# Turns by way of DRAM, and the forget gate's and the convolution's side work in smaller steps, in a hybrid decoder layer on one core

## The chip, the core and the metric

The kernel runs on one core of a Trainium2 chip. The metric is device time in microseconds (us), from launch to end. Three runs of the kernel before took 882.16, 876.36 and 881.53 us, a median of 881.53 us. One more execution was taken with the hardware profiler; all traces and tables here are of that one.

## The reference

One decoder layer, 256 tokens, model width 2048, all in float32:

```
h = rmsnorm(x)
c, b, xa, za, q, f, iv, og, ga, gb = split(h @ W_in)      # 8 x 1024 and 2 x 2048 columns
ya = b * causal_conv3(c * xa) * silu(za)                  # per column, three taps over tokens
lb = clip(lb_all, 0, 1 - 1e-6)
log_f = logaddexp(log(max(lb, 1e-30)), log1p(-lb) + log_sigmoid(f))
k  = (1 - lb) * sigmoid(-f)
o  = gated linear recurrence over tokens (silu(q), k, iv, log_f)   # 8 heads of 128, blocks of 64 tokens
yb = rmsnorm_per_head(o) * gain * silu(og)
m  = sigmoid(ga) * (ya @ W_a) + sigmoid(gb) * (yb @ W_b)
x  = x + m @ W_o
x  = x + sigmoid(rmsnorm(x) @ W_pg) * (p @ W_pp)
out = rmsnorm(x)
```

The result must be as exact as float32. TensorE has a fast format with fewer bits, so each factor is split into a high part (rounded to the fast format) and a low part (what is left), and a product is three matmuls: high x high, low weight x high, high weight x low activation.

## The kernel before

**Stream of weights.** All weights are read once, in 292 pieces called chunks here: 128 partitions x 1024 values, 512 KB. Two chunks come in one 1 MB transfer into a `raw` tile (three buffers, `load`, L104), issued on SyncE's queue. For each chunk `split` makes two halves: ScalarE copies `raw` to `whi` (L117, 1.05 us), then VectorE subtracts, `wlo = raw - whi` (L118, 1.24 us). Both have four buffers. TensorE then runs 12 matmuls of 128x512 on the chunk (`product`, L796 to L798), one every 0.227 us, 2.72 us in all. So each of the three engines has a job per chunk, and the next weights can be split only when the chunk four places earlier has been used up.

**Groups.** Chunks belong to groups, each with one product of two PSUM tiles (2 x 128 tokens, 512 columns). Their order: for j = 0 and 1 the groups f, q, iv, og, c, xa, za, b of 8 chunks each (chunks 0 to 127); for j = 0 to 3 ga and gb of 8, and A and B of 4 (128 to 223); O for j = 0 to 3 (224 to 255); then for j = 0 to 3 PP of one chunk and PG of 8.

**Side work.** After a group, its epilogue (`ep_f`, `ep_q`, `ep_xa`, ...) works on the result with VectorE, ScalarE, GpSimd and DMAs while TensorE is on the next groups. Epilogues are Python generators: the main loop advances each of them by one `yield` per chunk, and so a `yield` puts what stands behind it one chunk later. A scheduler then orders the instructions of each engine; within an engine they run strictly in that order, weight halves and side work in one queue. The recurrence itself (`hgrn`) is advanced in the same way.

**Turns.** A group's result has tokens on partitions. 18 tiles need columns on partitions instead: f, q, xa, b and yb (the recurrence's result) for j = 0 and 1; m (the merged branches) and x1 (the residual) for j = 0 to 3. VectorE's transpose turns 32x32 blocks within one quarter of the partitions, so the quarters must first be exchanged. `turned` (L178 to L196) does this with 16 transfers of 32 KB (32 partitions x 256 values) from SBUF to SBUF, issued one by one on SyncE's queue (L187), four or eight per `yield`; `lag` yields later comes the transpose (L194, 1.24 us). The weight loads are on the same queue and wait behind them.

**Forget gate.** `ep_f` turns f, takes two sigmoids of the turned tile (L239, L240), then for each of four heads scales `sn` into `kT` (L251) and takes three logarithms, with the scale `one` and the bias `low` of the lower bound inside the activation (L256); two of the three write 128x128 values, one 128x2. The scan (L259) sums the logarithms over 64 tokens; `tot` (L263, L264) and the `y` of the recurrence (L364) follow on VectorE. A sigmoid and a logarithm live in different tables of ScalarE; each change is a table load (1.28 us). q's epilogue, the next group, brings two sigmoids (L209) and two products (L226).

**Convolution.** `ep_xa` makes, for each of four blocks of 128x256, one VectorE multiplication for the last tap (L490) and seven shifted additions (L496), one block per `yield`.

**Late stages.** The four m tiles feed the groups O (`mh`, `ml`, L553 and L554); GpSimd adds the two merged halves (L549). `ep_o` adds O's result to the residual `xs` (L561), and turns it to x1 (`xh`, `xl`, L151 and L152) for PG.

Of the kernel before, what the change touches and what calls it, by code (L numbers as in the profile page):

```python
# [15 lines left out]
P = 128  # L16
# [28 lines left out]
def hybrid_kernel(ctx, tc, xT, x, pT, prm, gfin, masks, w_in, w_a, w_b, w_o, w_pg, w_pp, out):  # L45
# [4 lines left out]
    small = ctx.enter_context(tc.tile_pool(name="small", bufs=1))  # L50
    ps = ctx.enter_context(tc.tile_pool(name="ps", bufs=1, space=PSUM))
    big = ctx.enter_context(tc.tile_pool(name="big", bufs=1))


    pools, closers = {}, {}
# [21 lines left out]
    def t4(tag="t4", bufs=None):  # L77
        bufs = bufs or {"tmp1": 8, "tmp2": 5, "tmp3": 5}[state["tmp"]]
        return pools[state["tmp"]].tile([P, 1024], F32, tag=tag, bufs=bufs, name=nm(tag))
# [4 lines left out]
    def sc(n, tag="sc", bufs=12):  # L84
        return small.tile([P, n], F32, tag=tag, bufs=bufs, name=nm(tag))
# [89 lines left out]

        return ap.rearrange("p (b c t e) -> p t c b e", b=4, c=4, t=NT)[:, t]

    def turned(src, dst, step, lag):  # L178

        u = t4()
        for n in range(16):
            a, b = n % 4, n // 4
            nc.sync.dma_start(  # L187
                out=u[32 * b : 32 * b + 32, a * T : (a + 1) * T], in_=src[32 * a : 32 * a + 32, b * T : (b + 1) * T]
            )
            if n % step == step - 1:  # L190
                yield
        for _ in range(lag):
            yield
        nc.vector.transpose(  # L194
            out=dst.rearrange("p (k a e) -> p a k e", a=4, e=32), in_=u.rearrange("p (a k e) -> p a k e", a=4, e=32)
        )  # L196


    def scaled(psum, dst, turn=False):
# [34 lines left out]
    def ep_f(j, psum):  # L234
        fl = t4()
        scaled(psum, fl, True)
        yield from turned(fl, fl, 4, 3)
        sg, sn = t4(), t4()
        nc.scalar.activation(out=sg, in_=fl, func=AF.Sigmoid)  # L239
        nc.scalar.activation(out=sn, in_=fl, func=AF.Sigmoid, scale=-1.0)  # L240
        yield


        kT, lf, last = t4("kT", 1), t4(), sc(8, "lfl", 2)
        lv, sv = segments(lf), segments(sg)
        lsv = last.rearrange("p (h s) -> p h s", h=4)
        nc.gpsimd.memset(lv[:, :, 1, :, 0:1], 0.0)
        for h in range(4):
            s = slice(h * T, (h + 1) * T)
            one, low = (state[n][:, j * 4 + h : j * 4 + h + 1] for n in ("oml", "lbm"))  # L250
            nc.scalar.activation(out=kT[:, s], in_=sn[:, s], func=AF.Identity, scale=one)  # L251
            for to, fr in (
                (lv[:, h, 0], sv[:, h, 0]), (lv[:, h, 1, :, 1:], sv[:, h, 1, :, : SCAN - 1]),
                (lsv[:, h], sv[:, h, 1, :, SCAN - 1]),
            ):
                nc.scalar.activation(out=to, in_=fr, func=AF.Ln, scale=one, bias=low)  # L256
        yield
        b, tot = t4("b", 1), sc(16, "tot", 2)
        nc.vector.tensor_tensor_scan(  # L259
            out=b, data0=carry, data1=lf, initial=0.0, op0=ALU.mult, op1=ALU.add  # L260
        )
        bv, tv = segments(b), tot.rearrange("p (h k s) -> p h k s", h=4, k=2)
        nc.vector.tensor_copy(out=tv[:, :, 0], in_=bv[:, :, 0, :, SCAN - 1])  # L263
        nc.vector.tensor_tensor(  # L264
            out=tv[:, :, 1], in0=bv[:, :, 1, :, SCAN - 1],
            in1=last.rearrange("p (h s) -> p h s", h=4), op=ALU.add,
        )
        state["kT", j], state["b", j], state["tot", j] = kT, b, tot

    def ep_q(j, psum):  # L270
        sg, qt = t4(), t4()
        sig(psum, sg)
        plain_times(psum, sg, qt)
        qT = t4("qT", 1)
        yield from turned(qt, qT, 4, 3)
        state["qT", j] = qT

    def ep_iv(j, psum):
        v = t4("v", 1)
# [4 lines left out]
    def ep_og(j, psum):  # L284
        sg, o = t4(), t4("og", 1)
        sig(psum, sg)
        times(psum, sg, o)
        state["og", j] = o
        yield
        yield  # L290
        yield from hgrn(j)

    def hgrn(j):
# [144 lines left out]
        ss = sc(8, "ssh", 2)  # L438
        for n in range(8):
            t, h = n // 4, n % 4  # L440
            nc.scalar.activation(
                out=sq[:, n * P : (n + 1) * P], in_=o[t][:, h * P : (h + 1) * P], func=AF.Square,
                scale=state["rstd1"][:, t : t + 1], accum_out=ss[:, n : n + 1],
            )
# [5 lines left out]
        yield  # L450
        for n in range(8):
            t, h = n // 4, n % 4
            nc.scalar.activation(
                out=spread(sq, t)[:, h], in_=yb[:, n * P : (n + 1) * P].rearrange("p (b e) -> p b e", e=32),
                func=AF.Identity, scale=rh[:, n : n + 1],
            )
        yield from turned(sq, yb, 8, 3)
        for i in range(4):
            k = j * 4 + i
            put(state["ybT"], k, yb[:, i * T : (i + 1) * T], gain(PRM_GHG, k))  # L460
# [13 lines left out]
    def ep_xa(j, psum):  # L474
        cx = t4()
        plain_times(psum, state["c", j], cx)
        cxT = cx
        yield from turned(cx, cxT, 4, 3)
        cv = t4("cv", 1)
        for h in range(2):  # L480
            for i in range(2):
                n = h * 2 + i
                k = j * 4 + n
                d, s = cv[:, n * T : (n + 1) * T], cxT[:, n * T : (n + 1) * T]

                def w(tap):
                    c = PRM_CONV + tap * 8 + k
                    return prm_t[:, c : c + 1]

                nc.vector.tensor_scalar(out=d, in0=s, scalar1=w(2), scalar2=None, op0=ALU.mult)  # L490

                for tap, to, fr, n_ in (
                    (1, 1, 0, P - 1), (1, P, P + 1, P - 1), (1, T - 1, P - 1, 1),
                    (0, 2, 0, P - 2), (0, P, P + 2, P - 2), (0, T - 2, P - 1, 1), (0, T - 1, P - 2, 1),
                ):
                    nc.vector.scalar_tensor_tensor(  # L496
                        out=d[:, to : to + n_], in0=s[:, fr : fr + n_], scalar=w(tap), in1=d[:, to : to + n_],
                        op0=ALU.mult, op1=ALU.add,
                    )
                yield  # L500
        state["cv", j] = cv

    def ep_za(j, psum):
# [6 lines left out]
    def ep_b(j, psum):  # L510
        bz = t4()
        plain_times(psum, state["zs", j], bz)
        ya = bz
        yield from turned(bz, ya, 8, 3)
        nc.vector.tensor_tensor(out=ya, in0=state["cv", j], in1=ya, op=ALU.mult)
        yield
        hi, lo = (x[:, j * 4 : (j + 1) * 4, :].rearrange("p k t -> p (k t)") for x in state["yaT"])
        nc.scalar.activation(out=hi, in_=ya, func=AF.Copy)
        nc.vector.tensor_tensor(out=lo, in0=ya, in1=hi.bitcast(F32), op=ALU.subtract)
# [21 lines left out]
    def ep_bb(j, psum):  # L541
        ga, gb = state["ga", j], state["gb", j]
        for t in range(NT):
            s = slice(t * CW, (t + 1) * CW)
            nc.vector.tensor_tensor(out=gb[:, s], in0=gb[:, s], in1=psum[t], op=ALU.mult)  # L545
        m = t4()
        for t in range(NT):
            s = slice(t * CW, (t + 1) * CW)
            nc.gpsimd.tensor_tensor(out=spread(m, t), in0=blocks(ga[:, s]), in1=blocks(gb[:, s]), op=ALU.add)  # L549
        yield from turned(m, m, 8, 2)  # L550
        k = j * 4
        hi, lo = (x[:, k : k + 4, :].rearrange("p k t -> p (k t)") for x in state["mT"])
        nc.scalar.activation(out=hi, in_=m, func=AF.Copy)  # L553
        nc.vector.tensor_tensor(out=lo, in0=m, in1=hi.bitcast(F32), op=ALU.subtract)  # L554

    def ep_o(j, psum):
        xs = state["x"]
        src = t4()
        for t in range(NT):
            d = xs[:, t, j * CW : (j + 1) * CW]  # L560
            nc.vector.tensor_tensor(out=d, in0=d, in1=psum[t], op=ALU.add)  # L561
            nc.scalar.activation(  # L562
                out=src[:, t * CW : (t + 1) * CW], in_=d, func=AF.Square,
                accum_out=state["ss2"][:, t * 4 + j : t * 4 + j + 1],
            )
        x1 = src
        for t in range(NT):
            nc.scalar.activation(  # L568
                out=spread(x1, t), in_=blocks(xs[:, t, j * CW : (j + 1) * CW]), func=AF.Copy
            )  # L570
        yield from turned(x1, x1, 8, 2)
        for c in range(4):
            put(state["x1T"], j * 4 + c, x1[:, c * T : (c + 1) * T], gain(PRM_GPLE, j * 4 + c))
        if j == 3:
            tot = sc(2, "tot2", 1)
            nc.vector.tensor_reduce(
                out=tot, in_=state["ss2"].rearrange("p (t j) -> p t j", t=NT),
                axis=mybir.AxisListType.X, op=ALU.add,
            )
            state["rstd2"] = rsqrt_of(tot, NT, D, "r2")  # L580
# [374 lines left out]
```

## Time and profile before

| what | value |
|---|---|
| profiled execution, its own time | 880.19 us |
| span, first to last instruction | 878.4 us |
| mean granted TensorE clock | 0.982 |
| busy: TensorE, VectorE, ScalarE, GpSimd | 836.3, 527.6, 443.3, 77.0 us |
| idle time of TensorE between matmuls, and after the last | 33.5 and 8.5 us |
| instructions of VectorE, ScalarE | 592, 584 |
| bytes read from and written to HBM | 161.39 and 2.10 MB |
| DMA busy share of 16 engines, main queue | 55.5% |

The matmuls are a stream that is nearly always busy; the holes in it are these (start in the span, length, what ended the wait):

| place | start, length (us) | ended by | what stood before it |
|---|---|---|---|
| start | 0.00 1.45; 4.96 0.53; 8.87 1.11; 10.48 0.22 | warm-up, whi, wlo | first loads |
| A | 29.85 1.10; 31.69 0.53 | whi, wlo | scaling of f (L201) on ScalarE |
| B | 62.00 4.17; 67.39 3.00 | whi, wlo | first f: sigmoids, logarithms, scan |
| C | 227.83 1.04; 229.38 0.76; 236.10 0.28 | whi, wlo | 32 transfers of two turns, b and yb |
| D | 260.70 4.11; 266.02 3.00 | whi, wlo | second f |
| E | 426.19 1.00; 427.69 0.76; 434.45 0.24 | whi, wlo | as C, for j = 1 |
| F | 625.61 0.56 | wlo | a turn of m |
| G | 686.13 1.38; 688.24 0.53 | mh, ml | last turn of m, ahead of O |
| H | 715.81 4.24; 720.78 0.53 | whi, wlo | first turn of x1 |
| K | 785.37 2.27; 788.37 0.53 | xh, xl | last turn of x1, ahead of PG |

The granted clock is half of full speed from 65.7 to 76.0 us, 263.7 to 274.0, 721.1 to 724.5 and 789.4 to 792.8.

How to read the lines: an instruction group is named by line, engine, operation, and tiles out<-in. A row of a timeline is start in us, duration, engine, line, operation, tiles, count, and in brackets the idle time before and what ended it. A row of waits is the waiting engine and line, what it waited for, and total us, times, longest. A row of windows is the stretch, its length, then the busy us of PE, PEld, DVE, ACT and POOL (with instruction counts), the granted clock, the DMA share and GB/s. PE is TensorE, DVE VectorE, ACT ScalarE, POOL GpSimd, and SPq the queue of SyncE, on which most transfers are issued.

### The profile page before, as it was taken

The page shows a single profiled execution, that of the slowest core. Times are in us where ns is not written, and L with a number is a line of the kernel's source. Part 1 is how long each engine was busy: PE and PEld are TensorE (multiplying, and loading weights), DVE is VectorE, ACT ScalarE, POOL GpSimd, SP SyncE. Part 2 cuts the span into 40 slices and gives each one's busy share as a digit, 9 for nine tenths or more (in the row PEclk, how much of TensorE's full clock was granted, in tenths as well). Part 3 has the DMA queues.
Part 4 walks back from the last instruction along what each step waited for, and adds up shares of the span by engine and source line. Part 5 has one row for each costly group of instructions (what it writes and reads, how often), then busy time and mean ns, then how long its engine had stood idle before and what let it go on. Part 6 is the DMA issues. An engine that isn't in the chain of part 4 may idle for free. (4 is left out here: it accounts for less than half of the span.)

```text
span 878.4 us, 10033 instructions
## 1 busy us (share of the span) xinstructions
PE 836.3 (95%) x3753; PEld 687.4 (78%) x3753; DVE 527.6 (60%) x592; ACT 443.3 (50%) x584; POOL 77.0 (9%) x76
## 2 busy tenths in 40 slices
PE   8988999999988999999999999999999979989996
PEld 5766888888776888888788888888788768868885
DVE  7445586985646586985645545545545546655572
ACT  7673474445473474445443443443443445555552
POOL 1000032201000032200001001001001000001110
PEclk9997999999997999999999999999999999999999
DMA  9755645643654745643664753753753856554542
GB/s 334 292 197 172 235 164 180 209 166 101 224 204 141 265 153 188 212 155 111 229 242 139 273 200 128 275 200 123 269 200 131 338 198 250 192 201 160 207 153 96
DMA packets 39793, 173.59 MB, mean 198 GB/s; under 512 B 7616, under 2 KB 16832, under 8 KB 21568
## 3 DMA queue, kind: packets, MB, share of 16 engines
q1 hardware_dynamic: 39312, 172.39, 55.5%
q8 instruction: 29, 0.48, 0.2%
q10 hardware_dynamic: 432, 0.56, 0.2%
q14 instruction: 20, 0.16, 0.1%
HBM read 161.39 MB, written 2.10 MB: 186 GB/s over the span
## 5 line engine op out<-in xcount | busy, mean ns | idle before, releaser
L118 DVE TENSOR_TENSOR wlo<-raw,whi 128x1024 fp32r<-128x1024 f32 (+1 forms) x294 | 361.6, 1242 | 250.7 <-ACT whi L117 246.9
L117 ACT ACTIVATE whi<-raw 128x1024 fp32r<-128x1024 f32 (+1 forms) x294 | 305.4, 1052 | 319.7 <-PE g L798 272.8
L796 PE MATMUL g<-whi,xh 128*128 128x512 f32 (+1 forms) x912 | 355.6, 392 | 15.3 <-ACT whi L117 13.1
L797 PE MATMUL g<-wlo,xh 128*128 128x512 f32 (+1 forms) x912 | 356.0, 390 | 9.5 <-DVE wlo L118 9.4
L798 PE MATMUL g<-whi,xl 128*128 128x512 f32 (+1 forms) x912 | 354.4, 389 | 0.5 <-DVE xl L152 0.5
L796 PEld LDWEIGHTS g<-whi,xh 128*128 128x128 f32 x912 | 172.9, 190 | 52.9 <-ACT whi L117 16.1
L797 PEld LDWEIGHTS g<-wlo,xh 128*128 128x128 f32 x912 | 173.0, 190 | 48.7 <-DVE wlo L118 14.7
L798 PEld LDWEIGHTS g<-whi,xl 128*128 128x128 f32 x912 | 173.1, 190 | 35.5 <-DVE xl L152 1.0
L796 PE MATMUL g<-whi,mh 128*128 128x512 f32 x128 | 50.2, 393 | 5.6 <-ACT whi L117 4.2
L797 PE MATMUL g<-wlo,mh 128*128 128x512 f32 x128 | 50.7, 396 | 0.5 <-DVE wlo L118 0.5
L798 PE MATMUL g<-whi,ml 128*128 128x512 f32 x128 | 50.6, 395 | 0.5 <-DVE ml L554 0.5
L194 DVE STREAM_TRANSPOSE t<-t 128x1024 f32<-128x1024 f32 x16 | 19.9, 1241 | 39.6 <-DMA t<-t 39.6
L549 POOL TENSOR_TENSOR t<-ga,gb 128x512 f32<-128x512 f32 x8 | 14.1, 1789 | 255.5 <-DVE gb L545 192.8
L796 PEld LDWEIGHTS g<-whi,mh 128*128 128x128 f32 x128 | 24.2, 190 | 11.5 <-ACT whi L117 4.7
L797 PEld LDWEIGHTS g<-wlo,mh 128*128 128x128 f32 x128 | 24.4, 191 | 6.1 <-DVE wlo L118 1.0
L798 PEld LDWEIGHTS g<-whi,ml 128*128 128x128 f32 x128 | 24.5, 191 | 6.0 <-DVE ml L554 1.0
L796 PE MATMUL g<-whi,yaTh 128*128 128x512 f32 x64 | 24.9, 389 | 0.0
L797 PE MATMUL g<-wlo,yaTh 128*128 128x512 f32 x64 | 24.9, 389 | 0.0
L798 PE MATMUL g<-whi,yaTl 128*128 128x512 f32 x64 | 24.9, 389 | 0.0
L796 PE MATMUL g<-whi,ybTh 128*128 128x512 f32 x64 | 24.9, 389 | 0.0
L797 PE MATMUL g<-wlo,ybTh 128*128 128x512 f32 x64 | 24.9, 389 | 0.0
L798 PE MATMUL g<-whi,ybTl 128*128 128x512 f32 x64 | 24.9, 389 | 0.0
(147 smaller groups left out, 539.7 us busy)
## 6 DMA issues: line engine op xcount, KB each, us to landing
raw<-in_w_in SPq DMA_DIRECT2D x91, 1024.0 KB, 5.0
raw<-in_w_o SPq DMA_DIRECT2D x16, 1024.0 KB, 5.3
raw<-in_w_pg SPq DMA_DIRECT2D x16, 1024.0 KB, 4.9
t<-t SPq DMA_DIRECT2D x288, 32.0 KB, 1.9
raw<-in_w_a SPq DMA_DIRECT2D x8, 1024.0 KB, 5.0
raw<-in_w_b SPq DMA_DIRECT2D x8, 1024.0 KB, 5.0
raw<-in_w_in SPq DMA_DIRECT2D x9, 512.0 KB, 7.8
t<-in_xT SPq DMA_DIRECT2D x8, 256.0 KB, 7.5
```

The source lines that it names most:

```text
L117: nc.scalar.activation(out=hi[:, s], in_=src[:, s], func=AF.Copy)
L118: nc.vector.tensor_tensor(out=lo[:, s], in0=src[:, s], in1=hi[:, s].bitcast(F32), op=ALU.subtract)
L194: nc.vector.transpose(out=dst.rearrange("p (k a e) -> p a k e", a=4, e=32), in_=u.rearrange("p (a k e) -> p a k e", a=4, e=32))
L549: nc.gpsimd.tensor_tensor(out=spread(m, t), in0=blocks(ga[:, s]), in1=blocks(gb[:, s]), op=ALU.add)
L796: nc.tensor.matmul(psum, oh, hi, start=first, stop=False)
L797: nc.tensor.matmul(psum, oh, lo, start=False, stop=False)
L798: nc.tensor.matmul(psum, ol, hi, start=False, stop=last)
```

## The change

A new `turned` writes the four partition quarters of the tile to a DRAM tile (128 KB each, three such buffers), and reads it back in one transfer of 512 KB into the tile it came from; the transpose goes to a new tile, `lag` yields after. So five transfers replace 16, and the read waits for the writes. In `ep_f` the four scalings and the scale and bias of the logarithms become eight VectorE operations of 128x256, the logarithms become three activations over all heads (of 128x512, 128x504 and 128x8), and more `yield`s stand between the parts. In `ep_xa` the first multiplication goes to ScalarE, and the block's additions are spread over more chunks. `hgrn` gets two more `yield`s and `ep_og` one less; the lags of the turns of q, xa, yb, b, m and x1 change. The built order of the new program keeps the same matmuls, weight loads and weight halves; 288 issues of turns become 90.

```
--- before.py
+++ after.py
@@ -50,6 +50,7 @@
     small = ctx.enter_context(tc.tile_pool(name="small", bufs=1))
     ps = ctx.enter_context(tc.tile_pool(name="ps", bufs=1, space=PSUM))
     big = ctx.enter_context(tc.tile_pool(name="big", bufs=1))
+    dram = ctx.enter_context(tc.tile_pool(name="dram", bufs=1, space=bass.MemoryType.DRAM))
 
 
     pools, closers = {}, {}
@@ -175,25 +176,25 @@
 
         return ap.rearrange("p (b c t e) -> p t c b e", b=4, c=4, t=NT)[:, t]
 
-    def turned(src, dst, step, lag):
-        u = t4()
-        for n in range(16):
-            a, b = n % 4, n // 4
-            nc.sync.dma_start(
-                out=u[32 * b : 32 * b + 32, a * T : (a + 1) * T], in_=src[32 * a : 32 * a + 32, b * T : (b + 1) * T]
-            )
-            if n % step == step - 1:
-                yield
+    def turned(src, lag, dst=None):
+        d = dram.tile([P, 4, T], F32, tag="turn", bufs=3, name=nm("turn"))
+        to = d.rearrange("(b i) a x -> a i b x", b=4)
+        for a in range(4):
+            nc.sync.dma_start(out=to[a], in_=src[32 * a : 32 * a + 32, :].rearrange("i (b x) -> i b x", b=4))
+        yield
+        nc.sync.dma_start(out=src, in_=d.rearrange("p a x -> p (a x)"))
         for _ in range(lag):
             yield
+        dst = t4() if dst is None else dst
         nc.vector.transpose(
-            out=dst.rearrange("p (k a e) -> p a k e", a=4, e=32), in_=u.rearrange("p (a k e) -> p a k e", a=4, e=32)
-        )
+            out=dst.rearrange("p (k a e) -> p a k e", a=4, e=32), in_=src.rearrange("p (a k e) -> p a k e", a=4, e=32)
+        )
+        return dst
 
 
     def scaled(psum, dst, turn=False):
@@ -234,31 +235,46 @@
     def ep_f(j, psum):
         fl = t4()
         scaled(psum, fl, True)
-        yield from turned(fl, fl, 4, 3)
-        sg, sn = t4(), t4()
-        nc.scalar.activation(out=sg, in_=fl, func=AF.Sigmoid)
-        nc.scalar.activation(out=sn, in_=fl, func=AF.Sigmoid, scale=-1.0)
-        yield
-        kT, lf, last = t4("kT", 1), t4(), sc(8, "lfl", 2)
-        lv, sv = segments(lf), segments(sg)
-        lsv = last.rearrange("p (h s) -> p h s", h=4)
-        nc.gpsimd.memset(lv[:, :, 1, :, 0:1], 0.0)
+        sn = yield from turned(fl, 4)
+        sg = t4()
+        nc.scalar.activation(out=sg, in_=sn, func=AF.Sigmoid)
+        yield
+        nc.scalar.activation(out=sn, in_=sn, func=AF.Sigmoid, scale=-1.0)
+        kT = t4("kT", 1)
+        one, low = (state[n][:, j * 4 : j * 4 + 4] for n in ("oml", "lbm"))
         for h in range(4):
             s = slice(h * T, (h + 1) * T)
-            one, low = (state[n][:, j * 4 + h : j * 4 + h + 1] for n in ("oml", "lbm"))
-            nc.scalar.activation(out=kT[:, s], in_=sn[:, s], func=AF.Identity, scale=one)
-            for to, fr in (
-                (lv[:, h, 0], sv[:, h, 0]), (lv[:, h, 1, :, 1:], sv[:, h, 1, :, : SCAN - 1]),
-                (lsv[:, h], sv[:, h, 1, :, SCAN - 1]),
-            ):
-                nc.scalar.activation(out=to, in_=fr, func=AF.Ln, scale=one, bias=low)
+            nc.vector.tensor_scalar(
+                out=sg[:, s], in0=sg[:, s], scalar1=one[:, h : h + 1], scalar2=low[:, h : h + 1],
+                op0=ALU.mult, op1=ALU.add,
+            )
+        yield
+        for h in range(4):
+            s = slice(h * T, (h + 1) * T)
+            nc.vector.tensor_scalar(
+                out=kT[:, s], in0=sn[:, s], scalar1=one[:, h : h + 1], scalar2=None, op0=ALU.mult
+            )
+        yield
+        yield
+        lf, last = t4(), sc(8, "lfl", 2)
+        lv, fv = segments(lf), segments(sg)
+        nc.gpsimd.memset(lv[:, :, 1, :, 0:1], 0.0)
+        nc.scalar.activation(out=lv[:, :, 0], in_=fv[:, :, 0], func=AF.Ln)
+        nc.scalar.activation(
+            out=lv[:, :, 1, :, 1:], in_=fv[:, :, 1, :, : SCAN - 1], func=AF.Ln
+        )
+        nc.scalar.activation(
+            out=last.rearrange("p (h s) -> p h s", h=4), in_=fv[:, :, 1, :, SCAN - 1], func=AF.Ln
+        )
+        yield
         yield
         b, tot = t4("b", 1), sc(16, "tot", 2)
         nc.vector.tensor_tensor_scan(
             out=b, data0=carry, data1=lf, initial=0.0, op0=ALU.mult, op1=ALU.add
         )
+        yield
         bv, tv = segments(b), tot.rearrange("p (h k s) -> p h k s", h=4, k=2)
         nc.vector.tensor_copy(out=tv[:, :, 0], in_=bv[:, :, 0, :, SCAN - 1])
         nc.vector.tensor_tensor(
@@ -271,9 +287,7 @@
         sg, qt = t4(), t4()
         sig(psum, sg)
         plain_times(psum, sg, qt)
-        qT = t4("qT", 1)
-        yield from turned(qt, qT, 4, 3)
-        state["qT", j] = qT
+        state["qT", j] = yield from turned(qt, 5, t4("qT", 1))
 
     def ep_iv(j, psum):
         v = t4("v", 1)
@@ -286,7 +300,6 @@
         sig(psum, sg)
         times(psum, sg, o)
         state["og", j] = o
-        yield
         yield
         yield from hgrn(j)
 
@@ -438,6 +451,8 @@
         ss = sc(8, "ssh", 2)
         for n in range(8):
             t, h = n // 4, n % 4
+            if n == 4:
+                yield
             nc.scalar.activation(
                 out=sq[:, n * P : (n + 1) * P], in_=o[t][:, h * P : (h + 1) * P], func=AF.Square,
                 scale=state["rstd1"][:, t : t + 1], accum_out=ss[:, n : n + 1],
@@ -450,11 +465,13 @@
         yield
         for n in range(8):
             t, h = n // 4, n % 4
+            if n == 4:
+                yield
             nc.scalar.activation(
                 out=spread(sq, t)[:, h], in_=yb[:, n * P : (n + 1) * P].rearrange("p (b e) -> p b e", e=32),
                 func=AF.Identity, scale=rh[:, n : n + 1],
             )
-        yield from turned(sq, yb, 8, 3)
+        yb = yield from turned(sq, 3)
         for i in range(4):
             k = j * 4 + i
             put(state["ybT"], k, yb[:, i * T : (i + 1) * T], gain(PRM_GHG, k))
@@ -474,8 +491,7 @@
     def ep_xa(j, psum):
         cx = t4()
         plain_times(psum, state["c", j], cx)
-        cxT = cx
-        yield from turned(cx, cxT, 4, 3)
+        cxT = yield from turned(cx, 4)
         cv = t4("cv", 1)
         for h in range(2):
             for i in range(2):
@@ -487,17 +503,22 @@
                     c = PRM_CONV + tap * 8 + k
                     return prm_t[:, c : c + 1]
 
-                nc.vector.tensor_scalar(out=d, in0=s, scalar1=w(2), scalar2=None, op0=ALU.mult)
+                nc.scalar.activation(out=d, in_=s, func=AF.Identity, scale=w(2))
 
                 for tap, to, fr, n_ in (
                     (1, 1, 0, P - 1), (1, P, P + 1, P - 1), (1, T - 1, P - 1, 1),
                     (0, 2, 0, P - 2), (0, P, P + 2, P - 2), (0, T - 2, P - 1, 1), (0, T - 1, P - 2, 1),
                 ):
+                    if (tap, to) == (0, 2):
+                        yield
+                        yield
                     nc.vector.scalar_tensor_tensor(
                         out=d[:, to : to + n_], in0=s[:, fr : fr + n_], scalar=w(tap), in1=d[:, to : to + n_],
                         op0=ALU.mult, op1=ALU.add,
                     )
-                yield
+                if n < 3:
+                    yield
+                    yield
         state["cv", j] = cv
 
     def ep_za(j, psum):
@@ -510,8 +531,7 @@
     def ep_b(j, psum):
         bz = t4()
         plain_times(psum, state["zs", j], bz)
-        ya = bz
-        yield from turned(bz, ya, 8, 3)
+        ya = yield from turned(bz, 4)
         nc.vector.tensor_tensor(out=ya, in0=state["cv", j], in1=ya, op=ALU.mult)
         yield
         hi, lo = (x[:, j * 4 : (j + 1) * 4, :].rearrange("p k t -> p (k t)") for x in state["yaT"])
@@ -547,7 +567,7 @@
         for t in range(NT):
             s = slice(t * CW, (t + 1) * CW)
             nc.gpsimd.tensor_tensor(out=spread(m, t), in0=blocks(ga[:, s]), in1=blocks(gb[:, s]), op=ALU.add)
-        yield from turned(m, m, 8, 2)
+        m = yield from turned(m, 3)
         k = j * 4
         hi, lo = (x[:, k : k + 4, :].rearrange("p k t -> p (k t)") for x in state["mT"])
         nc.scalar.activation(out=hi, in_=m, func=AF.Copy)
@@ -568,7 +588,7 @@
             nc.scalar.activation(
                 out=spread(x1, t), in_=blocks(xs[:, t, j * CW : (j + 1) * CW]), func=AF.Copy
             )
-        yield from turned(x1, x1, 8, 2)
+        x1 = yield from turned(x1, 3)
         for c in range(4):
             put(state["x1T"], j * 4 + c, x1[:, c * T : (c + 1) * T], gain(PRM_GPLE, j * 4 + c))
         if j == 3:
```

## The prediction

> **What bounds the kernel now.** The page first: TensorE is busy 95% of the span, and its clock row has a 7 and an 8 in it, so the kernel is one stream of matmuls, and only TensorE's holes and its slow stretches can be won back.
>
> ```profile
> PE 836.3 (95%) x3753; PEld 687.4 (78%) x3753; DVE 527.6 (60%) x592; ACT 443.3 (50%) x584; POOL 77.0 (9%) x76
> PEclk9997999999997999999999999999999999999999
> ```
>
> The waits of TensorE, by releaser, come next. The halves of the weights (whi on ScalarE, wlo on VectorE) end 27 of its 33.5 us of holes; the last two rows are turned tiles that arrive late.
>
> ```profile
> PE g L796 <- ACT whi L117: 17.3, 8, 4.2
> PE g L797 <- DVE wlo L118: 9.9, 10, 3.0
> PE g L796 <- ACT xh L151: 2.3, 1, 2.3
> PE g L796 <- ACT mh L553: 1.4, 1, 1.4
> ```
>
> Why is whi late? ScalarE around the hole at 62.00 us answers for the first f.
>
> ```profile
> 54.34 1.04 ACT L117 ACTIVATE whi<-raw 128x1024 fp32r<-128x1024 f32 x1
> 55.29 0.49 ACT L251 ACTIVATE kT<-t,lc 128x256 f32<-128x256 f32 x1
> 55.79 1.28 ACT L256 ACT_TABLE_LOAD   x1
> 57.09 0.88 ACT L256 ACTIVATE t<-t,lc,lc 128x128 f32<-128x128 f32 x2
> ...
> 62.61 1.28 ACT L209 ACT_TABLE_LOAD   x1
> 63.90 1.27 ACT L209 ACTIVATE t<-g,r1r 128x512 f32<-128x512 f32 x2
> 65.06 2.00 ACT L117 ACTIVATE whi<-raw 128x1024 fp32r<-128x1024 f32 x2
> ```
>
> From 55.29 to 65.06 there is no copy of weights. A copy may run from the end of the fourth chunk before and is needed at the end of the last one before it, three chunks or 8.2 us later, less its own 1.0: an absence of 9.8 us cannot be covered. TensorE stands 4.17 us; then VectorE, which runs scan, tot, y and two q products in a row (62.41 to 69.12), brings wlo late by another 3.00.
>
> The queue of SyncE gives the other cause: the 16 issues of a turn at about 0.6 us each stand ahead of a weight load.
>
> ```profile
> 206.93 15.08 SPq L187 DMA_DIRECT2D t<-t  x24
> 222.11 0.53 SPq L104 DMA_DIRECT2D raw<-in_w_in  x1
> ```
> ```profile
> 703.02 10.71 SPq L187 DMA_DIRECT2D t<-t  x16
> 713.83 1.48 SPq L104 DMA_DIRECT2D raw<-in_w_o  x3
> ```
>
> The first of these loads lands at 227.66 and TensorE stops at 227.83; the second lands at 718.86, TensorE has stopped at 715.81. Last the windows after the two f holes: the mean clock is 0.77.
>
> ```profile
> 66.00:88.00 22.00, 18.83 (x68) 14.85 (x69) 12.48 (x11) 8.22 (x10) 0.92 (x1) 0.77 0.51 175
> 264.00:286.00 22.00, 18.19 (x67) 14.34 (x68) 13.08 (x12) 8.51 (x10) 1.56 (x2) 0.77 0.45 152
> ```
>
> **A loss per place.** A chunk takes 12 matmuls at 0.227 us, 2.72 us. What a stretch took over its chunks' 2.72 is its loss, slow clock included. B (first f): chunks 19 to 23 end at 62.00 + 24.45, 24.45 - 13.6 = 10.85. D (second f): 10.5. C and E (turns of b and yb, at 227.83 and 426.19): 2.08 and 2.0. F (turn of m, 625.61): 0.56. G (last turn of m, 686.13): 1.9. H (first turn of x1, 715.81): 28.63 for eight chunks, 6.9. K (last turn of x1, 785.37): 10.44 for two, 5.0. At the start and at A (29.85, 1.63) 5 us, untouched.
>
> **The change part by part.**
>
> *Turns.* 16 issues become 4 writes and a read. The row of 16 is 10.71 us; four of the 0.59 us kind and one of the loads' 0.33 to 0.53 are 2.9. So the 18 turns give SyncE's queue 7.8 us back each. At C, E and F loads that were 2.1, 2.0 and 0.6 us late go out 8 to 16 us earlier: all of 4.6 us is won. But the read waits on SyncE until the four writes have landed, and the next weight load is queued behind it. The trace has no write to DRAM of this size: below it, 32 KB turns land after 1.9 us; above, 256 KB stores of the result after 2.3 and 256 KB loads after 3.5; behind a 1 MB weight load, 5.0. The nearest row is the store; I take 2.3 alone, 5.0 where a load lies ahead. The read is 512 KB: the pp load's 3.7, plus 2.5 (spacing of back-to-back 1 MB loads) behind one. A turn then takes 2.4 + 2.3 + 0.5 + 3.7 = 8.9 us up to 14, against 10.7 + 1.9 = 12.6 now. One to two chunks more of waiting are covered by the lags: a transpose stands 4 to 6 chunks (11 to 16 us) after its writes.
>
> How long may SyncE be blocked? A weight buffer comes free some 2.3 us after the chunk three before it ends; the load takes 5.0; the built order leaves 11.3 us from there, and the copies lead by another 5.8: about 12 us. Blocked time is 2.4 issues + 2.3 to 5.0 + 0.5, so 5 to 8: hidden.
>
> [...]
>
> *Forget gate.* Per j eight logarithms of 0.48, four of 0.37 and four scalings of 0.49 leave ScalarE (7.3 us), three logarithms come: two of half a tile, at the 0.67 of a 128x512 pass, and one of 0.37, so 1.7. VectorE gets eight 128x256 operations at L490's 0.344, 2.8 us. In the built order ScalarE has a weight copy between the sigmoids, q's sigmoids and the logarithms: the longest absence is a table load and three logarithms, 3.0, under the 7.1 that are covered. VectorE's longest row is four scalings plus q's products, 4 x 0.34 + 1.27 = 2.6, or the scan, 2.3, against 6.8 now. Walking chunk by chunk I find 2.5 us of slack at the first f and only 0.5 at the second (wlo of chunk 84, behind the scan). B and D go: 21.35 us, slow clock included.
>
> *Convolution.* Four L490 (0.344) per j go from VectorE to ScalarE at L251's 0.49, and the rest is spread; no hole lies there now, slack 1.5 us: nothing, at worst 4 x 0.5 = 2 us late less 1.5, twice, 1 us.
>
> *End stretches.* G: the tile is made at 673.72 by GpSimd. Four issues to 676.1, landed 678.4, a load ahead of the read: back at 682 to 683 against 685.0; and the built order puts half of the next chunk's matmuls first. 1.5 to 1.9 won. H: the load goes out some 10 us earlier, in time; but the built order has the two additions into xs, which wait for the last matmul of O1, ahead of wlo of chunk 240 on VectorE. That leaves a new stop of about 1.5 us: 6.9 - 1.5 = 5.4. K: pp's matmuls now stand ahead of the late half, 5.0 less 0.2 = 4.8.
>
> The clock is part of these sums. The granted clock is 0.5 for 10.24 us after B and D, and for 3.41 after H and K; after A, C and E (holes of 1.6 to 1.8 us in all) never. I count the new 1.5 us of H among these. [...]
>
> **Sum.** 10.85 + 10.5 + 4.6 + 1.7 + 5.4 + 4.8 = 37.9. The profiled execution took 880.2 us (span 878.4 and 1.8 around it): 842.3. The median of the runs, 881.5, stands 1.3 above it, so **843**. The case spans 836 (A, G, H and K wholly gone, as low as the fastest run before, 5 under its median) to 849.
>
> **Rivals.**
> 1. *The second f keeps a hole.* For: slack 0.5 against walked rows whose sizes are read off others; VectorE gets more work. Against: ScalarE's copies are well apart. If it passes 3 us, D stays with its 10.5: 853.5.
> 2. *The trip is late in the end stretches.* For: a load is queued between writes and read and waits for its buffer, up to 5.4 us. Then G, H and K, whose next matmuls need the turned tile, win nothing: 11.9 back, 855. With rival 1 also, 865.
> 3. *No net gain.* Transposes stand at the head of VectorE's queue; now 39.6 us of its idle time end with a turn's landing. If the read is later than the lags, wlo behind them is late, at all of the 18 turns by some 2 us: 36 back, 879. Against: the 14 us above.
> 4. *Slower.* The read's wait holds weight loads on SyncE. From 12 us of blocking on, each further us stops TensorE in every turn; with writes that land after 12 us, blocked time is 14.9, 2.9 x 18 = 52 against 38 won: 895. It loses from 14.1 us on. For: the longest landing of a 32 KB turn now is 8.8 us, behind other transfers. Against: that is the maximum of 288, their median 1.9.
>
> **Chances.** The forecast 0.57, rival 1 0.14, rival 2 0.15, rival 3 0.05, rival 4 0.09. One per cent, 8.8 us, is what a measurement of this kernel can tell: faster 0.57 + 0.14 + 0.15 = 0.86, same 0.05, slower 0.09. The range goes from 836 to 862, which takes in rivals 1 and 2, one at a time.
>
> **What the profile after would show.** Right: no hole over 1 us near 62 and 260, clock row without the 7; five issues per turn; the wait on whi down from 17.3 to under 5; a hole of about 1.5 us near 690, where O1 ends. Wrong: SyncE's waits before the read over 8 us, idle time of VectorE before the transposes well over 39.6, a 0.5 clock after the second f.

## The result and the profile after

Four runs of the changed kernel have a median of 840.39 us (839.47 to 841.24); the kernel before has 878.94 in the four runs beside them. The ratio is 0.956, with a 95% interval of 0.9515 to 0.9605. The profiled execution took 841.12 us, its span 839.3. Forecast were 843, between 836 and 862.

The page of the changed kernel, its busy row, the clock row and the chain that ended last:

```profile
PE 824.9 (98%) x3753; PEld 683.5 (81%) x3753; DVE 532.1 (63%) x600; ACT 433.2 (52%) x562; POOL 85.4 (10%) x76
PEclk9999999999999999999999999999999999999998
...
PE 96%; issue 1%; DMA 1%; DVE 1%; ACT 1%; SPq 0%; POOLq 0%; POOL 0%; ACTq 0%
```

TensorE is busy 98% of the span instead of 95%, and the two 7s in the clock row are gone. The chain that ends last is followed back to the start, and 96% of the span is TensorE itself. Before, the chain could be followed back only to 607 us; of that part, 267 us, TensorE was 54% (16% of the span). The waits of TensorE are these two rows, besides 1.5 us of warm-up at the start:

```profile
PE g L817 <- DVE wlo L119: 2.2, 3, 1.5
PE g L816 <- ACT whi L118: 1.9, 3, 1.1
```

From 27.2 us on the two weight halves to 4.1, and no wait on a turned tile (`xh`, `mh`). The issues of the turns, from the last part of the page (tiles, engine, count, size, median us to landing):

```profile
turn<-t SPq DMA_DIRECT2D x72, 128.0 KB, 2.6
t<-turn SPq DMA_DIRECT2D x18, 512.0 KB, 4.6
```

ScalarE at the first f, by its timeline (the forget gate's second sigmoid and its three logarithms are left out): a weight copy stands after the first sigmoid and another before the table load, and the longest absence is 2.5 us (57.16 to 59.63; 3.0 reckoned) where it was 9.8.

```profile
53.07 1.04 ACT L118 ACTIVATE whi<-raw 128x1024 fp32r<-128x1024 f32 x1
...
54.97 1.24 ACT L210 ACTIVATE t<-g,r1r 128x512 f32<-128x512 f32 x2
56.10 1.06 ACT L118 ACTIVATE whi<-raw 128x1024 fp32r<-128x1024 f32 x1
57.18 1.28 ACT L264 ACT_TABLE_LOAD   x1
...
59.63 2.04 ACT L118 ACTIVATE whi<-raw 128x1024 fp32r<-128x1024 f32 x2
```

And SyncE's queue at the turns of b and yb, where a weight load stood behind 24 issues:

```profile
198.70 1.78 SPq L188 DMA_DIRECT2D turn<-t  x4
200.58 0.38 SPq L105 DMA_DIRECT2D raw<-in_w_in  x1
203.37 0.34 SPq L190 DMA_DIRECT2D t<-turn  x1
```

A weight load now stands between a turn's writes and its read. Place by place, with one rule for both traces: whatever the start of a matmul lies later after the one before it than 0.227 us (0.115 for the half-width ones) is loss, holes and slow clock together.

| place | before (us) | after (us) | won | forecast |
|---|---|---|---|---|
| start | 2.34 | 1.83 | 0.5 | 0 |
| A | 2.18 | 3.78 | -1.6 | 0 |
| B, first f | 10.81 | 0 | 10.8 | 10.85 |
| C and E | 2.90 + 2.82 | 0 | 5.7 | 4.1 |
| D, second f | 10.44 | 0 | 10.4 | 10.5 |
| F | 0.84 | 0 | 0.8 | 0.56 |
| G | 2.45 | 0 | 2.5 | 1.7 |
| H | 6.81 | 1.73 | 5.1 | 5.4 |
| K | 4.94 | 0 | 4.9 | 4.8 |
| everything | 48.58 | 9.47 | 39.1 | 37.9 |

39.1 us is also what lies between the two profiled executions, 880.19 and 841.12. The rule counts a little more than the holes as listed: at C 2.90 us where the holes are 2.08, since a hole begins only at the modelled end of the last matmul.

### The profile page after: what moved, and what is told of

Its sections match the earlier page's. It is cut to its first block, busy times and chain, and to the rows that moved or that the text cites. A ratio compares the mean times of both kernels' runs of the same rounds, so it can differ in the third digit from the quotient of the medians.

```text
span 839.3 us, 9789 instructions
## 1 busy us (share of the span) xinstructions
PE 824.9 (98%) x3753; PEld 683.5 (81%) x3753; DVE 532.1 (63%) x600; ACT 433.2 (52%) x562; POOL 85.4 (10%) x76
## 4 chain that ended last, share of the span: by engine, by line
PE 96%; issue 1%; DMA 1%; DVE 1%; ACT 1%; SPq 0%; POOLq 0%; POOL 0%; ACTq 0%
PE g L817 31%; PE g L818 31%; PE g L816 31%; PE s L324 1%; DMA raw<-in_w_in 1%; PE s L433 0%; DVE wlo L119 0%; PE s L446 0%; PE s L445 0%; PE s L444 0%; ACT whi L118 0%; ACT xs L656 0%; ACT t L639 0%; SPq L709 0%; SPq L702 0%
## 5 line engine op out<-in xcount | busy, mean ns | idle before, releaser
L119 DVE TENSOR_TENSOR wlo<-raw,whi 128x1024 fp32r<-128x1024 f32 (+1 forms) x294 | 369.9, 1265 | 248.0 <-ACT whi L118 246.8
L817 PE MATMUL g<-wlo,xh 128*128 128x512 f32 (+1 forms) x912 | 352.3, 386 | 0.8 <-DVE wlo L119 0.8
L370 POOL TENSOR_TENSOR t<-b 128x512 f32<-128x512 f32 x10 | 17.5, 1776 | 65.8 <-DMA turn<-t 33.9
```

What stands on the lines that cost most here:

```text
L119: nc.vector.tensor_tensor(out=lo[:, s], in0=src[:, s], in1=hi[:, s].bitcast(F32), op=ALU.subtract)
L370: nc.gpsimd.tensor_tensor(out=er, in0=br, in1=ref, op=ALU.subtract)
L817: nc.tensor.matmul(psum, oh, lo, start=False, stop=False)
```

## The experiments

The later runs were compared with the kernel before on their own chip. Excess below means the loss by the rule of the table; before has 48.58 in all, after 9.47.

**Only the turns.**

```diff
 # the changed kernel, ep_f and ep_xa as before, but with the new turned
-    yield from turned(fl, fl, 4, 3)
+    fl = yield from turned(fl, 4)
     ... two sigmoids and 16 more activations per j, as before
```

> The changed kernel with the forget gate and the convolution as they were before: of the change only the turns by way of DRAM (and the two yields of the recurrence) are left. By the sum on record the gate is worth 21.4 us (B 10.85, D 10.5) and the convolution nothing: 841 + 21.4 = 862, two stops of about 4 and 3 us near 62 and 240 to 260, half clock behind each for some 10 us, and C, E, F, G, K gone. Rival: the burst was late only because the turn ahead of it was long, so that with five transfers it hides: 841 to 845.

Measured: 854.5 us (853.8 to 855.6), 0.973 of before (0.971 to 0.976), 23 us won instead of 16. Both f windows still stop TensorE, but B costs 6.95 us and D 5.26, not 10.8 and 10.4: at B holes of 1.75 and 2.75 and 6.83 us of half clock, where there had been 4.17, 3.00 and 10.24. The rows of ScalarE show why. Before, the burst began late, since the transpose that it needs was late; a weight copy before it had waited 3.73 us for a load as well:

```profile
47.79 2.01 ACT L117 ACTIVATE whi<-raw 128x1024 fp32r<-128x1024 f32 x2 [3.73 <-DMA raw<-in_w_in]
...
52.43 1.06 ACT L239 ACTIVATE t<-t 128x1024 f32<-128x1024 f32 x1 [1.33 <-DVE t L194]
```

With the turns alone the first sigmoid runs at 50.93, and a weight copy comes between the logarithms and q's sigmoids:

```profile
50.93 1.06 ACT L240 ACTIVATE t<-t 128x1024 f32<-128x1024 f32 x1
...
60.06 1.04 ACT L118 ACTIVATE whi<-raw 128x1024 fp32r<-128x1024 f32 x1
61.12 1.28 ACT L210 ACT_TABLE_LOAD   x1
```

So B and D were the burst's, but 9 of their 21 us hung on the turn as well; neither the forecast's account (all the gate's) nor the rival (none) was right.

**Only the gate.**

```diff
 # the kernel before, ep_f as changed, turned as before
-    sn = yield from turned(fl, 4)
+    sn = fl
+    yield from turned(fl, fl, 4, 3)
```

> The kernel before with the new forget gate alone; turns in 16 transfers, convolution as before. By the sum on record only B and D go: 880 - 21.4 = 859, with C, E, F, G, H and K as they were. Rival: the gate needs the shorter turn (its own turned tile comes later by SBUF); then a stop of 1 us or more stays near 62 and 260 and the time is 865 or more.

Measured: 857.7 us (855.7 to 858.4), 0.977 (0.973 to 0.980), 20 us won. No hole is left at B or D, and C, E, G, H and K stand about as before, by the gaps of TensorE: 0.89 and 0.76 at 216.74, 1.01 and 0.76 at 405.50, 1.38 at 665.26, 3.95 at 694.96, 1.89 at 764.26. F has shrunk to 0.17 at 605.16. This came as expected. By the excess of the traces the turns alone win 25.8, the gate alone 23.3, both with the convolution 39.1. The two parts together are 10.0 more than the whole; 9 us of that are those of B and D, which either part removes and which are counted twice. By the medians it is 23, 20 and 38 to 39.

**The convolution undone.**

```diff
-                nc.scalar.activation(out=d, in_=s, func=AF.Identity, scale=w(2))
+                nc.vector.tensor_scalar(out=d, in0=s, scalar1=w(2), scalar2=None, op0=ALU.mult)
 # and one yield per block, as before
```

> The changed kernel with the convolution as before (first tap on VectorE, a block per chunk). The sum on record has it at nothing: 841, no stop of TensorE at the convolution (150 to 185 and 340 to 375 us). In the trace after, weight halves there are ready 4.3 us or more ahead of their use, and 4 x 0.34 us more on VectorE fit into that. Rival: the eight new VectorE operations of the gate and the quicker turns had made VectorE tight, and the convolution had to be spread: 843 or more, with stops there.

Measured: 841.77 us (841.6 to 843.6), 0.959 (0.957 to 0.962). Its trace has two holes that the changed kernel has not, at 174.49 and 360.67:

```profile
PE s L433 <- DVE kT L423: 2.0, 2, 1.0
```

They are not weight halves: the recurrence's own small matmuls wait for `kT`, which on VectorE stands behind a block's seven additions.

```profile
173.50 1.51 DVE L512 SCALAR_TENSOR_TENSOR cv<-t,prm_t,cv 128x127 f32<-128x127 f32 x7
174.93 0.75 DVE L423 TENSOR_TENSOR kT<-kT,t 128x256 f32<-128x256 f32 x2
```

They lose 1.24 us each by the table's rule, 2.5 in all; by the medians it is 1.4, and the 95% intervals of the two ratios overlap. So in the changed kernel the spreading of the convolution is worth 1 to 3 us. In the kernel before, the unspread convolution has no such hole: `kT` was ready at 180.42 and first used at 187.82. In the changed one, where the recurrence has other `yield`s, 2.0 us lie between, and with the convolution undone none.

**Seventeen transfers through DRAM.**

```diff
-            nc.sync.dma_start(out=to[a], in_=src[32 * a : 32 * a + 32, :].rearrange("i (b x) -> i b x", b=4))
+            for b in range(4):
+                nc.sync.dma_start(out=to[a][:, b, :], in_=src[32 * a : 32 * a + 32, b * T : (b + 1) * T])
```

> The changed kernel with each 128 KB write to DRAM cut into four of 32 KB: 16 writes and a read, 17 transfers per turn. Same bytes, same trip. If it is the issues on SyncE's queue that made weight loads late, 12 more of 0.45 to 0.6 us, 5.4 to 7.2 us per turn, bring stops back at the turns of b and yb and at the last stages: 2 to 5 us for C, E and F, up to 5 each at H and K, 846 to 856. If the order of the work or the way through DRAM is what counts: 841.

Measured: 850.65 us (848.9 to 851.6), 0.969 (0.966 to 0.972); 10 us of the gain are gone, with the same bytes by the same way. SyncE's queue at b and yb:

```profile
197.25 7.29 SPq L189 DMA_DIRECT2D turn<-t  x16
204.63 0.37 SPq L105 DMA_DIRECT2D raw<-in_w_in  x1
...
206.27 9.42 SPq L189 DMA_DIRECT2D turn<-t  x16
215.79 0.36 SPq L105 DMA_DIRECT2D raw<-in_w_in  x1
```

Holes come back after these loads (0.53 at 223.10), at 410, 661 (1.13 and 0.53) and 691 (1.78 and 0.42). Two more (0.52 at 245.71, 0.21 at 251.77) have no late load behind them; they stand at the second f. So what counts in the main is the time that issues ahead of a load take on its queue, and not the way through DRAM.

**A longer trip.** One more copy, DRAM to DRAM, and three more:

```diff
+        d2 = dram.tile([P, 4, T], F32, tag="hop0", bufs=3, name=nm("hop"))
+        nc.sync.dma_start(out=d2, in_=d)
+        d = d2
         nc.sync.dma_start(out=src, in_=d.rearrange("p a x -> p (a x)"))
```

> The changed kernel with one more transfer in each turn: DRAM tile copied to a second DRAM tile, 512 KB, before it is read back; SyncE waits for that too. Trip 9.5 us in the median plus about 4.5, so 14, as in the run with 17 transfers; SyncE blocked some 9 us from the first issue to the read's, under the 12 of the sum on record. So weight loads stay in time, and only transposes that had less than 4.5 us of slack come late: 843 to 852. If blocking hurts from the first us on: 18 turns by 4.5 us, 81 on top, 920.

> The changed kernel with three more copies from DRAM to DRAM in each turn, one waiting for the other on SyncE. Trip about 9.5 + 13.5 = 23 us, SyncE blocked about 18: 6 beyond the 12 that the last rival of the prediction reckons with. By that rival every turn then stops TensorE by some 6 us: 840 + 18 x 6 = 948, slower than before. If the cover is much longer than 12 us, only the late transposes show: 855 to 880.

One copy more: 839.2 us (838.4 to 839.9), 0.955 (0.952 to 0.958), no slower than the change itself and under the 843 to 852 that were expected. A trip, from its first issue to the landing of the read, takes 15.1 us in the median; 9.4 in the changed kernel, 12.3 before and 14.7 with 17 transfers. So the length of the trip costs nothing up to there, and a trip of 14.7 us that begins with 16 issues costs 10. SyncE shows the difference:

```profile
213.01 0.47 SPq L191 DMA_DIRECT2D hop<-turn  x1
213.53 0.58 SPq L105 DMA_DIRECT2D raw<-in_w_in  x1
217.30 0.33 SPq L193 DMA_DIRECT2D t<-hop  x1
```

The waits are few, each for some 4 us, and weight loads go out between them. In this program the built order also has the additions behind the low half of chunk 240, and the hole near 686 is not there. Three copies more: 894.2 us in its one execution, 16 slower than before and between the two sums expected, with trips of 23 to 36 us. But not by the road of the last rival: no weight load is issued more than 8.8 us after its buffer came free. The waits of TensorE name the turned tile of the last stages:

```profile
PE g L825 <- ACT xh L152: 36.5, 3, 21.7
```

**How late a weight load may be.** From the traces: a load's issue, less the end of the low half that frees its buffer, beside the hole that TensorE has for it.

| run, place | issued late by (us) | hole (us) |
|---|---|---|
| before, turns of m at 487 and 552 | 11.3 | none |
| before, F | 12.4 | 0.56 |
| before, C, first and second load | 12.3; 14.4 | 1.04 + 0.76; 0.28 |
| gate alone, at 531 and 598 | 11.3; 12.1 | 0.28; 0.17 |
| before, H | 17.4 | 4.24 + 0.53 |
| seventeen, at 216 and 404 | 12.9; 13.3 | 0.53; 0.18 + 0.53 |
| seventeen, at 687 | 14.9 | 1.78 + 0.42 |
| seventeen, at 657 | 8.6 | 1.13 + 0.53 |
| after, largest | 7.5 | none by the load |
| one copy more, largest | 8.3 | none |

At 11.3 us there is no hole or a small one, from 12.1 on there is always one: the cover is 11 to 12 us, and the prediction had 12. The last row of the run with 17 transfers is the exception. By the count of its matmuls TensorE has done 230 chunks there and asks for chunk 232, as chunks 230 and 231 need the last m tile, which was not there yet (`mh` at 665.21). A chunk that is wanted two places, or 5.4 us, early has that much less cover.

**Another queue.** Two runs issue 16 transfers from SBUF to SBUF on GpSimd, in the kernel before and in the changed one:

```diff
-            nc.sync.dma_start(
+            nc.gpsimd.dma_start(
                 out=u[32 * b : 32 * b + 32, a * T : (a + 1) * T], in_=src[32 * a : 32 * a + 32, b * T : (b + 1) * T]
             )
 # second run: the same 16 in the new turned, all before its first yield
```

> The kernel before with the 16 transfers of a turn issued on GpSimd's queue instead of SyncE's; still from SBUF to SBUF, gate and convolution as before. If weight loads were late only because 16 issues stood ahead of them on SyncE's queue, C, E and F go and H shrinks to a rest of 1.5 us: 2.9 + 2.8 + 0.8 + 5 off 878, 866. B and D stay; G and K hang on the trip, which this leaves as it is or lengthens (GpSimd issues at its own pace). Rival: the small transfers themselves hold up the loads in the DMA engines; then C, E, F and H stay and the time is 877 or more.

> The changed kernel with its turns not through DRAM: 16 transfers of 32 KB inside SBUF again, issued on GpSimd's queue; gate, convolution and lags as changed. It tells whether DRAM is needed, or only a free queue for the weight loads. In the run with GpSimd's queue alone no weight load was late by over 4 us. If the free queue is all, 841 to 845. If the slower trip of 16 transfers counts (transposes that wait at the head of VectorE's queue with weight halves behind them, and the last stages), stops come at the turns as they did there (0.8 to 2.5 us at 228, 424, 677, 733, 753): 848 to 856.

The first: 867.8 us (866.7 to 871.8), 0.989 (0.985 to 0.992), and no weight load is late by over 4 us. The total came as forecast, its parts did not. C, E, F and H in their old form are gone, but new stops appear (2.52 at 423.79, 1.39 at 732.77, 2.31 at 753.64), and B and D are smaller. The second: 865.8 us (863.8 to 867.6), 0.986 (0.983 to 0.989), 26 us over the changed kernel and past the range of its rival. VectorE's waits and the issues on GpSimd say where (of a line: who waited, us, times; landing min/median/max):

```profile
  DVE t L195: 84.1, 16
...
DMA to landing us min/median/max: 1.7/4.0/7.6
```

VectorE stands 84.1 us before transposes for a landing (39.6 before the change, 0.2 in the changed kernel), and low halves queue behind them: TensorE waits 14.8 us for these. A free queue for the loads is not enough; a turn must also have landed when VectorE comes to it. GpSimd, at 0.50 us an issue and 4.0 to landing, gives only the first. Whether a turn inside SBUF with fewer and larger transfers would do as well as DRAM was not run.

**The last hole, and a control.**

```diff
     def ep_o(j, psum):
+        for _ in range(3):
+            yield
         xs = state["x"]
```

> The changed kernel as it is, beside the two that follow and on their chip. 840.4 us by the runs so far, 0.956 of before; in its runs two groups 1.7 us apart (839.5 and 841.2), since the stop at A has half clock behind it in some and not in others.

> The changed kernel with three yields at the start of the epilogue of O, so that in the built order the two additions into the residual that wait for O1's last matmul stand behind the low half of chunk 240 instead of ahead of it. If the stop of 1.46 us near 686 is that order alone, it goes and the time is 1.5 us lower, 838.9, nothing else changed. If what is late there is the weight load (7.5 us after its buffer was free) or the turn, the stop stays or moves: 840.4 or more.

The changed kernel again: 839.69 us (839.4 to 840.9), 0.9564 (0.954 to 0.9588). With the later additions 839.78 (839.6 to 841.6), 0.9567 (0.9543 to 0.9591): the same, and not the 838.9 expected. But the cause of the hole was named rightly. In the changed kernel VectorE stands before it, waits for O1's last matmul, does the two additions, and only then the low half that TensorE needs:

```profile
685.45 1.37 DVE L581 TENSOR_TENSOR xs<-xs,g 128x512 f32<-128x512 f32 x2 [7.88 <-PE g L818]
686.73 1.22 DVE L119 TENSOR_TENSOR wlo<-raw,whi 128x1024 fp32r<-128x1024 f32 x1
```

With the other order that hole is gone, and a new one stands in the last turn of x1:

```profile
753.01 0.73 PE L818 MATMUL g<-whi,xh 128*128 128x512 f32 x2 [1.63 <-ACT whi L118]
```

**Which stop costs clock.** In the changed kernel A has 3.41 us of half clock behind it, in the repeat it has none. Two runs stop TensorE by repeated weight copies on ScalarE, which leave the results as they are:

```diff
-        nc.scalar.activation(out=hi[:, s], in_=src[:, s], func=AF.Copy)
+        for _ in range({134: 10, 150: 11, 168: 12, 186: 13, 204: 15}.get(pos, 1)):
+            nc.scalar.activation(out=hi[:, s], in_=src[:, s], func=AF.Copy)
 # second run: ten chunks, 6 or 7 copies
```

> The changed kernel with the ScalarE copy of chunks 134, 150, 168, 186 and 204 repeated 10, 11, 12, 13 and 15 times (0.95 us each), so that TensorE stops at each by about 1.3, 2.3, 3.2, 4.2 and 6 us plus 0.5 for the other half. What half clock follows which stop? By the sum on record none after a stop under 2 us, 3.41 us after 2.3 to 4, 10.24 after one of 4 with another behind it. [...] Time 840 + 17 of stops + 5 to 12 of slow clock, 862 to 870.

> The changed kernel with the ScalarE copy of ten chunks (134 to 215, every ninth) repeated 6 or 7 times, for ten stops of some 1 to 3 us; by the earlier run with 10 copies (5.6 us) a copy less is 0.95 us less. The slow stretches of all runs so far begin and end on a grid of 3.413 us. In their windows the first half clock follows a window in which TensorE stood 2.0 us or more in every case, 1.56 or less in none, and in six of eight between 1.61 and 1.88. If that is the rule, each of these stops has half clock behind it exactly when 1.6 to 1.9 us or more of it lie in one window, so that a stop of 2 us cut in two by the grid has none. [...] If chance, there is no such order.

The first took 894.4 us, past the 862 to 870 expected: the stops were longer than planned (5.57, 5.85, 8.25, 9.39 and 11.46 us). Side work among the copies is a part of it; the rest was not followed up. Behind them came 6.83, 10.24, 10.24, 10.24 and 13.65 us at half clock, counted from within the stop: 2, 3, 3, 3 and 4 times 3.413. All slow stretches of a run (but the tail's ends) begin a whole number of 3.413 us after one another; those of before 0, 58, 192 and 212 times that after the first. The second run (860.2 us) had stops from 0.2 to 2.3 us. Cut into windows of that length, counted from the slow stretches of the run:

```profile
471.40:474.80 3.40, 1.39 (x6) 0.66 (x4) 0.58 (x1) 3.40 (x5) 0.00 (x0) 1.00 0.00 0
474.80:478.20 3.40, 2.88 (x7) 2.15 (x7) 3.40 (x4) 1.28 (x2) 0.00 (x0) 0.50 0.51 147
...
526.00:529.40 3.40, 2.79 (x13) 1.98 (x11) 0.00 (x0) 3.37 (x4) 0.00 (x0) 1.00 0.49 142
529.40:532.80 3.40, 2.33 (x9) 1.63 (x10) 2.88 (x3) 1.44 (x2) 0.00 (x0) 1.00 0.38 104
532.80:536.30 3.50, 3.50 (x17) 2.90 (x16) 3.50 (x4) 1.62 (x2) 0.00 (x0) 1.00 0.96 398
```

After the stretch, PE's busy us come first and the clock is the third from the end. The stop of 2.01 us at 472.23 fell into one window (3.40 less 1.39) and has half clock behind it, 6.83 us by the clock record. The stops of 1.15 and 0.53 at 528.79, 1.68 together, were cut by the windows into 0.61 and 1.07, and have none. Both are as expected for idle time within one window (half clock from 1.6 to 1.9 us on).

## Why the prediction was right, point by point

**What bounds the kernel** held: only holes and slow stretches were won, and 39.1 us of them answer for all of the time. (One row was misread: the clock row before has two 7s, not a 7 and an 8.)

**Turns.** Five issues take 2.1 us in most turns (1.78 for four writes, 0.34 for the read), less than the 2.9 reckoned. Writes land after 2.6 us in the median, between the 2.3 and 5.0 taken (7.4 at most); the read after 4.6, within 3.7 to 6.2 (8.0 at most); the trip is 8.8 to 12.8, against 8.9 to 14. From the first write to the read SyncE needs 4.3 to 8.1 us, 5 to 8 reckoned, and its longest wait for the writes is 4.7. By the two medians write and read take 7.2 us in series, against 6.0 reckoned with no load ahead (2.3 and 3.7), and TensorE has no wait on a turned tile. The cover of 12 us was nearly right by the table of late loads. What the term mis-sized is the share: turns alone won 23 us, not 16.5, since 9 us of B and D hung on the late turn too. The sum did not suffer, as the same loss was there to be won once.

**Gate.** Right: no hole at either f. By the trace the low half of chunk 20 is ready 3.2 us before its use (2.5 reckoned) and that of chunk 84 1.5 (0.5). Rival 1 hung on this slack and did not come.

**Convolution.** As a term of the sum "nothing" is right: neither kernel has a hole there. What was overlooked is that the other parts of the change bring the recurrence's `kT` close to the convolution, so that without the spreading 1 to 3 us would have been lost; slack was reckoned for weight halves only.

**End stretches.** G and K as reckoned (K's matmuls are ahead of its late half), H with its rest: 1.5 us forecast, 1.46 measured, and named by its cause.

**Clock.** "After A, C and E never" is true of the trace before and not of all runs. The trace after has 3.41 us at half behind A, the run with the gate alone has it behind C (0.89 and 0.76). Half of 3.41 us is 1.7, and so far apart are the two groups in the runs of the changed kernel (839.5 and 841.2).

**Sum.** That 37.9 came within 1.2 us of 39.1 is in part luck. C, E, F and G were sized by their holes and lost more than these, 2.7 us in all by the table's rule; the half clock behind A took 1.6 of that back. The last step is also off by a little: 842.3 and 1.3 are 843.6, not 843.

**Rivals.** The second (a late trip) did not come: G, H and K were won, and even one copy more cost nothing. The third (transposes waiting at the head of VectorE's queue) is not in the change, 0.2 us, but is what the runs on GpSimd show. The fourth, slower than before, exists from some length of trip between 15 and 26 us (the medians with one copy more and with three) on; its place is the last stages and not the weight loads: with three copies more, loads still go out between two copies and none is over 8.8 us late, while behind 16 or 24 issues some were 12 to 17 us late.

## What to carry to other kernels

Count what stands ahead of a prefetch on its queue, in issues and not in bytes: 16 small transfers of 0.6 us each made loads late that five larger ones, with more bytes and a way through DRAM, did not. Before pricing a burst of side work, work out the cover in the trace (here an estimated 7 us for a weight half, from three chunks of 2.72 less a copy of 1.05, and 11 to 12 for a load by the table of late loads) and break the burst so that no engine is away from the stream for longer. Ask of such a repair what each part wins alone: two causes of one hole count it twice.

## What was not expected of the hardware

In the traces of before and after the slow stretches, but for the tail's, are 3.41 or 10.24 us long, one or three times 3.413, and their starts lie a whole number of 3.413 us apart. Cut into windows of that length, each trace by its own slow stretches, the idle time of TensorE in a window (by the ends of matmuls that the profile models) goes with the clock of the next one. Over all 14 traces (before, after and the runs above), of windows at full clock after the start: with 0.3 to 1.56 us idle, 89 of 89 were followed by full clock; with 1.61 to 1.88, 9 of 12 by half; with 2.0 or more, 19 of 19. Between 1.56 and 2.0 us these traces draw no sharp line, and what sets the clock was not shown. Both one hole (2.01 us in the run with small stops) and two (1.10 and 0.53, at A in the trace after) brought half clock. The same two holes at A lay in one window after (1.63 us idle, 3.78 us lost by the table) and in two windows before (2.18 us lost).
